# Encoder trunk on one core: neighbourhood values as one Strassen product, softmax division on ScalarE, two strips of w_out cut ahead

## The chip, the cores and the metric

The kernel runs on one core of one Trainium2 chip. Its engines are named as in the profile: PE is TensorE's matmul (PEld its weight load), DVE is VectorE, ACT is ScalarE, POOL is GpSimd, SP is SyncE, which here only issues DMAs. The metric is the device time of one launch in microseconds; lower is better.

## The reference

Two layers act on x, 256 rows of 2048 numbers. Each adds first a mixture of two attentions, then an MLP:

```
u = rmsnorm(x, norm_mix[l]);  proj = u @ w_in[l]
c_q, c_kv, k_pe, q_na, k_na, v_na, gate_a, gate_b = split(proj)
y_a = mla_attention(...) @ w_o_mla[l]                # 8 heads of latent attention, from c_q, c_kv, k_pe
y_b = neighbourhood_attention(q_na, k_na, v_na, rpb[l]) @ w_o_na[l]   # 8 heads of 128
x = x + (sigmoid(gate_a) * y_a + sigmoid(gate_b) * y_b) @ w_out[l]
x = x + square(relu(rmsnorm(x, norm_mlp[l]) @ w_ff1[l])) @ w_ff2[l]
```

and a last rmsnorm. Everything is float32. The values of the neighbourhood attention, `v_na`, are 1024 columns of `u @ w_in`, 128 for each of its 8 heads. A neighbourhood head computes scores from its queries and keys, adds a learned bias and a mask, takes a softmax over the 256 keys, and multiplies by its values.

## The kernel before

**A float32 product is made of three.** Every weight and activation is split into `hi`, rounded to the short float that TensorE multiplies (fp32r), and `lo`, the remainder; a product is hi x hi + lo x hi + hi x lo, three matmuls into one PSUM bank. ACT makes `hi` (lines 176 and 197), DVE `lo` (177 and 198). A weight is loaded as a block of 1 MB into one of 3 `raw` buffers by a DMA of SP. There are 8 PSUM banks, shared by all, and 51 slots of SBUF for activations.

**Kinds of product.** `gemm_b` gives 512 columns with the output turned, in 4 banks (lines 354, 359); `gemm_a` gives 512 columns by `group_a` (306, 310) in 2 banks, 16 row tiles x 2 x 3 = 96 matmuls of 128x512 where the input has 2048 columns; `gemm_s` (537) gives 1024 columns and runs over 8 pairs of row tiles, in the order `[0, 4, 1, 5, 2, 6, 3, 7]`. An ordinary pair costs 24 matmuls in 4 banks. Pairs 1, 2 and 3 (`MIXED`, `MERGED`) go by Strassen: 7 instead of 8 block products, 21 matmuls, in 7 banks. For that DVE forms `sums` of the weights (574 to 578), which are then split too, and `forms` prepares sums of the activations. At the end ACT and DVE put the quadrants together from the banks (587 and 586).

**The order.** The first layer runs `gemm_first` over all 1024 query columns of the neighbourhood part; the second layer makes the queries in two halves. Then, for each half of four heads: keys (`C_KN`, gemm_b), values (`C_VN`, two banks, `group_a`), and the four heads go into `queued`. Next come `C_Q`, `C_KV`, the rotary key, then the gates (`C_GB`, `C_GA`, gemm_s), `w_o_na`, the latent heads, `w_o_mla` (four gemm_a of 512 columns), `w_out` (two gemm_s) and the MLP.

**Heads run between products.** A head is a generator. Products call `tick()` now and then; every 6 ticks a queued head starts, and it yields between its steps: scores (three matmuls for each half, lines 314 to 316 in the old numbering, then `s` on DVE, 717), softmax (`nmx`, 650; exp on ACT, 658; `inv`, 662; the division `p` x `inv`, 664), 13 ticks later four transposes into a bank (669) and their split into `pp` on ACT and DVE (671, 672), 3 ticks later six value matmuls into another bank, split into `pair` (165, 167). A scheduler that orders each engine's instructions ahead of time has the last word, within the data's dependencies; at run time each engine takes its own list strictly in that order.

**Stores.** The first half of a layer uses `wpool` (4 buffers each of hi and lo, 1024 wide) and `tmp`; `half_a.close()` at line 910 gives both back before `w_out`, and `wpool2` (4 buffers, 2048 wide) with `tmp2` takes the space for `w_out` and the MLP.

## Time and profile before

| | |
|---|---|
| three runs | 2600.32, 2600.32, 2599.18 us; median 2600.32 |
| profiled run | 2599.52 us, of which the span (first to last instruction) is 2597.7 |
| PE busy | 2585.0 us, 100% of the span, 12432 matmuls |
| DVE busy | 2176.4 us, 84% |
| ACT busy | 1487.5 us, 57% |
| POOL busy | 98.0 us, 4% |
| read from HBM | 494.28 MB, 191 GB/s over the span |
| granted TensorE clock | 0.999 |

A page of the profile gives busy time by engine, the chain of work that ended last, and groups of equal instructions with the mean duration of one. Matmuls are pipelined, so the record of one is longer than its share of the engine. A group's line ends with the idle time of its engine just before it, and what ended that idle time. A row of the timeline has the start in us, the duration, engine, line, operation, output <- inputs, and, in brackets, the idle time before it and its releaser.

### The profile page before, as it was taken

What the parts mean: (1) busy time and instruction counts of PE and PEld (TensorE: products, weight loads), DVE (VectorE), ACT (ScalarE), POOL (GpSimd) and SP (SyncE); (2) the same over time, 40 slices, a digit from 0 to 9 for tenths busy, and PEclk for the clock granted to TensorE, in tenths of its full rate; (3) what the DMA queues carried; (4) which work ended last, traced back from release to release, by engine and by line L of the source; (5) the groups of instructions that cost most, each with busy time, mean ns of one, the idle gap of its engine ahead of it and who ended that gap; (6) DMA issues with size and microseconds to landing.
All of it is one profiled execution on the core that took longest, in us unless ns stands there. A gap on an engine that the chain in (4) does not pass through costs nothing.

```text
span 2597.7 us, 32260 instructions
## 1 busy us (share of the span) xinstructions
PE 2585.0 (100%) x12432; PEld 2171.9 (84%) x12432; DVE 2176.4 (84%) x2538; ACT 1487.5 (57%) x1732; POOL 98.0 (4%) x118
## 2 busy tenths in 40 slices
PE   9999999999999999999999999999999999999998
PEld 8888889888888888888888888898888888888887
DVE  7778889699988898888667788896999988988885
ACT  6555557456655645546545555574666556555463
POOL 0200000000000010000001000000000000100000
PEclk9999999999999999999999999999999999999999
DMA  7655564555577585675565555645656765856754
GB/s 266 217 171 195 180 205 151 165 191 195 195 219 220 176 259 198 202 239 171 178 201 178 173 194 182 205 149 161 197 180 211 234 199 192 246 194 209 243 180 145
DMA packets 173994, 511.06 MB, mean 197 GB/s; under 512 B 13840, under 2 KB 18832, under 8 KB 173584
## 3 DMA queue, kind: packets, MB, share of 16 engines
q1 hardware_dynamic: 164640, 491.78, 57.1%
q0 software_dynamic: 8768, 16.78, 3.3%
q8 instruction: 97, 1.59, 0.2%
q10 hardware_dynamic: 432, 0.43, 0.1%
q14 instruction: 57, 0.47, 0.1%
HBM read 494.28 MB, written 2.10 MB: 191 GB/s over the span
## 4 chain that ended last, share of the span: by engine, by line
PE 99%; issue 0%; ACT 0%; DVE 0%; POOL 0%; DVEq 0%; POOLq 0%; ACTq 0%
PE bank L537 67%; PE bank L306 8%; PE bank L354 6%; PE bank L310 4%; PE bank L359 3%; PE bank L285 2%; PE bank L507 1%; PE bank L260 1%; PE bank L286 1%; PE bank L314 1%; PE bank L316 1%; PE bank L315 1%; PE bank L258 1%; PE bank L669 1%; PE bank L605 0%
## 5 line engine op out<-in xcount | busy, mean ns | idle before, releaser
L537 PE MATMUL bank<-hi,pair 128*128 128x512 f32 x5124 | 1283.4, 390 | 2.1 <-ACT hi L176 2.1
L537 PEld LDWEIGHTS bank<-hi,pair 128*128 128x128 f32 x5124 | 958.0, 188 | 202.5 <-ACT hi L176 2.9
L176 ACT CAST hi<-raw 128x2048 fp32r<-128x2048 f32 (+3 forms) x416 | 622.7, 1517 | 301.7 <-PE bank L537 165.3
L177 DVE TENSOR_TENSOR lo<-raw,hi 128x2048 fp32r<-128x2048 f32 (+3 forms) x416 | 741.6, 1796 | 63.8 <-ACT hi L176 42.2
L537 PE MATMUL bank<-lo,pair 128*128 128x512 f32 x2562 | 697.2, 390 | 0.0
L537 PEld LDWEIGHTS bank<-lo,pair 128*128 128x128 f32 x2562 | 479.7, 188 | 99.4
L176 ACT CAST hi<-sums 128x2048 fp32r<-128x2048 f32 (+1 forms) x150 | 244.9, 1638 | 297.5 <-DVE sums L578 168.9
L177 DVE TENSOR_TENSOR lo<-sums,hi 128x2048 fp32r<-128x2048 f32 (+1 forms) x150 | 290.7, 1948 | 101.2 <-ACT hi L176 58.2
L198 DVE TENSOR_TENSOR lo<-raw,hi 128x1024 fp32r<-128x1024 f32 (+1 forms) x208 | 248.8, 1201 | 102.9 <-ACT hi L197 99.5
L197 ACT CAST hi<-raw 128x1024 fp32r<-128x1024 f32 (+1 forms) x208 | 214.1, 1035 | 205.0 <-PE bank L306 87.6
L306 PE MATMUL bank<-hi,pair 128*128 128x512 f32 x960 | 245.2, 392 | 0.0
L586 DVE TENSOR_TENSOR wide<-wide,bank 128x512 f32<-128x512 f32 x336 | 214.9, 679 | 6.5 <-PE bank L537 6.4
L306 PEld LDWEIGHTS bank<-hi,pair 128*128 128x128 f32 x960 | 178.3, 188 | 35.8
L354 PE MATMUL bank<-pair,hi 128*128 128x512 f32 x640 | 168.8, 395 | 0.0
L574 DVE TENSOR_TENSOR sums<-raw 128x1024 f32<-128x1024 f32 x126 | 153.7, 1220 | 13.9 <-DMA raw<-in_w_ff 7.3
L310 PE MATMUL bank<-lo,pair 128*128 128x512 f32 x480 | 131.9, 391 | 0.0
L354 PEld LDWEIGHTS bank<-pair,hi 128*128 128x128 f32 x640 | 112.4, 189 | 17.7
L310 PEld LDWEIGHTS bank<-lo,pair 128*128 128x128 f32 x480 | 89.4, 188 | 18.0
L516 ACT CAST pair<-wide 128x512 fp32r<-128x512 f32 x110 | 68.2, 620 | 59.8 <-DVE wide L475 57.5
L359 PEld LDWEIGHTS bank<-pair,lo 128*128 128x128 f32 x640 | 89.4, 190 | 7.2
L359 PE MATMUL bank<-pair,lo 128*128 128x256 f32 x640 | 93.7, 283 | 0.0
L578 DVE TENSOR_TENSOR sums<-raw,sums 128x512 f32<-128x512 f32 x126 | 86.6, 687 | 2.0
(165 smaller groups left out, 1890.7 us busy)
## 6 DMA issues: line engine op xcount, KB each, us to landing
raw<-in_w_ff SPq DMA_DIRECT2D x256, 1024.0 KB, 5.4
raw<-in_w_in SPq DMA_DIRECT2D x120, 1024.0 KB, 5.1
raw<-in_w_out SPq DMA_DIRECT2D x32, 1024.0 KB, 5.6
raw<-in_w_o_na SPq DMA_DIRECT2D x16, 1024.0 KB, 5.0
raw<-in_w_o_mla SPq DMA_DIRECT2D x16, 1024.0 KB, 5.0
xt<-wide POOLq DMA_DIRECT2D x48, 256.0 KB, 5.3
raw<-in_w_in SPq DMA_DIRECT2D x17, 512.0 KB, 5.6
raw<-in_w_ukv SPq DMA_DIRECT2D x8, 1024.0 KB, 5.0
```

Of the source, the lines that this page charges most:

```text
L176: nc.scalar.copy(hi, src)
L177: nc.vector.tensor_tensor(lo, src, hi.bitcast(F32), op=ALU.subtract)
L197: nc.scalar.copy(hi, src)
L198: nc.vector.tensor_tensor(lo, src, hi.bitcast(F32), op=ALU.subtract)
L306: nc.tensor.matmul(ps[t], a, wh[:, k], start=k0 + k + i == 0, stop=False)
L310: nc.tensor.matmul(ps[t], sides(have(acts, k0 + k), t)[0], wl[:, k], start=False, stop=k0 + k == nk - 1)
L354: nc.tensor.matmul(ps[m], wh[:, k, m * P:(m + 1) * P], have(acts, k0 + k), start=k0 + k == 0, stop=False)
L359: nc.tensor.matmul(ps[m][:, :S], wl[:, k, m * P:(m + 1) * P], have(acts, k0 + k)[:, :S], start=False, stop=k0 + k == nk - 1)
L537: nc.tensor.matmul(b[i], x, y, start=count[i] == 1, stop=count[i] == total[i])
L574: nc.vector.tensor_tensor(ts[0].rearrange("p (a n) -> p a n", a=2), raw[:, :512].rearrange("p (a n) -> p a n", a=1).to_broadcast([P, 2, 512]),
L578: final = nc.vector.tensor_tensor(t4, raw[:, 1536:], t2, op=ALU.subtract)
L586: add = lambda o, a, c: nc.vector.tensor_tensor(o, a, c, op=ALU.add)
```

## The change

Three edits.

1. **Values.** The two products `C_VN` of 512 columns become one `gemm_s` of 1024 columns with the pairs 1, 2, 3 by Strassen; `values` then reads the finished `wide` tiles instead of the banks. The values of all eight heads are made ahead of the second half of the keys. The `forms` of x, which the gates used first, move to the start of the layer; the loads of `xt` (the 2 MB of x, on SP) move behind the values.
2. **Division.** `p` x `inv` moves from DVE (`tensor_scalar_mul`) to ACT (a copy with a scale for each row).
3. **Strips ahead.** `cut` and the loading of a strip (`two_rows`) leave `gemm_s` and become functions of their own. A generator `strips_ahead`, started with the last `w_o_mla` product, closes `tmp`, opens a pool `wpool3` of two buffers on its space, and loads and cuts the first two strips of `w_out`; `gemm_s` takes them by its new argument `made`. From there on whole strips use `wpool3` and `wpool2` (2 buffers each) by turns, two strips from one, two from the other.

```diff
-        lo, hi = (wpool.tile([P, 2048 if strips else 1024], F32R, tag=tag, name=tag,
-                             bufs=hbufs)[:, :src.shape[-1]] for tag in ("lo", "hi"))
+        if strips:
+            whole_strips[0] += 1
+        pool, n, bufs = (stores[whole_strips[0] // 2 % 2], 2048, 2) if strips else (wpool, 1024, HBUFS)
+        hi, lo = (pool.tile([P, n], F32R, tag=tag, name=tag, bufs=bufs)[:, :src.shape[-1]] for tag in ("hi", "lo"))
...
+    def cut(src):
+        out, step = [], 2048 if strips else 1024
+        for c in range(0, src.shape[-1], step):
+            hi, lo = parts(src[:, c:min(c + step, src.shape[-1])])
+            out += [(hi[:, i:i + 512], lo[:, i:i + 512]) for i in range(0, hi.shape[-1], 512)]
+        return out
+
+    def two_rows(w, c0, j):
+        raw = raws.tile([P, 2048], F32, tag="raw", name="raw", bufs=RBUFS)
+        nc.sync.dma_start(raw.rearrange("p (k n) -> p k n", n=1024),
+                          w[2 * j * P:(2 * j + 2) * P, c0:c0 + 1024].rearrange("(k p) n -> p k n", p=P))
+        return raw
+
+    def gemm_s(w, c0, get, order, pairs, evac, made={}):
...
         first = next(j for j in order if j in pairs)
         for j in order:
-            raw = raws.tile([P, 2048], F32, tag="raw", name="raw", bufs=RBUFS)
-            nc.sync.dma_start(raw.rearrange("p (k n) -> p k n", n=1024),
-                              w[2 * j * P:(2 * j + 2) * P, c0:c0 + 1024].rearrange("(k p) n -> p k n", p=P))
+            raw = None if j in made else two_rows(w, c0, j)
             if j not in pairs:
-                ws = cut(raw)
+                ws = made[j] if j in made else cut(raw)
...
-            nc.vector.tensor_scalar_mul(p[:, b], p[:, b], inv[:, b:b + 1])
+            nc.scalar.activation(p[:, b], p[:, b], AF.Copy, scale=inv[:, b:b + 1])
...
+        qn, kn, xs4 = [None] * 8, [None] * 8, [None] * (NC // 2)
+
+        def put(norm, dst, g):
+            evac = to_pair(norm, dst)
+            return lambda m, ps: evac(g * 4 + m, ps)
+
+        def values_of(r):
+            return [[values(r[t, g], mix.col, t) for t in range(2)] for g in range(2)]
+
+        if l == 0:
+            gemm_first(wi, C_QN, xg, xf4, to_pair(None, qn), squared)
+            start(forms(xf4, MIXED, xs4), 8)
+            gemm_b(wi, C_KN, xg, put(mix, kn, 0), scaled, weights(wi, NC, C_KN, 512, tc.keep_in_program_order))
+            tables()
+        else:
+            start(forms(xf4, MIXED, xs4), 4)
+            gemm_b(wi, C_QN, xg, put(None, qn, 0), scaled)
+            gemm_b(wi, C_KN, xg, put(mix, kn, 0))
+        mixed, vt = blocks(xg, xs4, MIXED), []
+        gemm_s(wi, C_VN, mixed, ORDER, MIXED, lambda r: vt.extend(values_of(r)))
+        if l == 0:
+            for t in range(2):
+                tc.keep_in_program_order(nc.sync.dma_start(xt[t], x[t * P:(t + 1) * P]))
         for g in range(2):
-            qn, kn = (qn[4:] if l == 0 and g else [None] * 4), [None] * 4
-            if l == g == 0:
-                qn = [None] * 8
-                gemm_first(wi, C_QN, xg, xf4, to_pair(None, qn), squared)
-                gemm_b(wi, C_KN, xg, to_pair(mix, kn), scaled, weights(wi, NC, C_KN, 512, tc.keep_in_program_order))
-                tables()
-            else:
-                if l == 0:
-                    for t in range(2):
-                        tc.keep_in_program_order(nc.sync.dma_start(xt[t], x[t * P:(t + 1) * P]))
-                else:
-                    gemm_b(wi, C_QN + g * 512, xg, to_pair(None, qn), scaled if g == 0 else None)
-                gemm_b(wi, C_KN + g * 512, xg, to_pair(mix, kn))
-            ps = [bank() for _ in range(2)]
-            for k0, wh, wl in weights(wi, NC, C_VN + g * 512, 512):
-                group_a(ps, xg, k0, NC, wh, wl)
-                tick()
-            vt = [values(ps[t], mix.col, t) for t in range(2)]
-            for j in range(4):
-                h = g * 4 + j
-                queued.append(na_head(l, h, qn[j], kn[j], vt, mix.query, setter(att_na, h)))
+            if g:
+                if l:
+                    gemm_b(wi, C_QN + 512, xg, put(None, qn, 1))
+                gemm_b(wi, C_KN + 512, xg, put(mix, kn, 1))
+            for h in range(g * 4, g * 4 + 4):
+                queued.append(na_head(l, h, qn[h], kn[h], vt[g], mix.query, setter(att_na, h)))
...
+        half_b, made = ExitStack(), {}
+
+        def strips_ahead(l=l, made=made, half_b=half_b, heads_end=heads_end):
+            nonlocal strips
+            heads_end.close()
+            stores[0] = half_b.enter_context(tc.tile_pool(name="wpool3", bufs=2, side="right",
+                                                          reuse_waits="tile"))
+            whole_strips[0] = -1
+            for j in ORDER[:2]:
+                strips = True
+                made[j] = cut(two_rows(w_out[l], 0, j))
+                strips = False
+                if j == ORDER[0]:
+                    stores[0].tile([P, 56], F32, name="phase", bufs=1)
+                yield 1
...
+            if c4 == 3:
+                start(strips_ahead(), 7)
             gemm_a(w_o_mla[l], c4 * 512, att, merge)
...
+        while len(made) < 2:
+            tick()
         half_a.close()
...
-        wpool = half_b.enter_context(tc.tile_pool(name="wpool2", bufs=4, reuse_waits="tile"))
-        tmp = half_b.enter_context(tc.tile_pool(name="tmp2", bufs=2, reuse_waits="tile"))
+        wpool = stores[1] = half_b.enter_context(tc.tile_pool(name="wpool2", bufs=2, reuse_waits="tile"))
...
-            gemm_s(w_out[l], g * 1024, blocks(mg, ms4, MERGED), ORDER, MERGED, residual)
+            gemm_s(w_out[l], g * 1024, blocks(mg, ms4, MERGED), ORDER, MERGED, residual, {} if g else made)
```

In all, PE issues 18 matmuls of 128x512 fewer; 64 instructions move from DVE to ACT; 16 DMAs of 1 MB keep their bytes and change their shape. Three places show how the engines' lists move. In the names, `bank` is a PSUM bank and the number tells one tile from another; a wait in brackets names the engine or the DMA queue waited for.

**PE at the end of the second half of the keys, layer 0.** Before, `bank_999` to `bank_1002` are the key product, `pp_1220` and `bank_1271` belong to heads 1 and 2:

```order
L314 MATMUL bank_1241<-pp_1220,vh_989 128x256 [waits Activation_49]
L354 MATMUL bank_1002<-pair_458,hi_1263 128x512
L669 MATMUL bank_1271<-ident_71,p_1137 128x128 [waits DVE_49]
L669 MATMUL bank_1271<-ident_71,p_1137 128x128 x3
L354 MATMUL bank_999<-pair_461,hi_1263 128x512
L354 MATMUL bank_1000<-pair_461,hi_1263 128x512
L354 MATMUL bank_1001<-pair_461,hi_1263 128x512
L354 MATMUL bank_1002<-pair_461,hi_1263 128x512
L359 MATMUL bank_999<-pair_458,lo_1264 128x256
L359 MATMUL bank_999<-pair_461,lo_1264 128x256
L359 MATMUL bank_1000<-pair_458,lo_1264 128x256
L315 MATMUL bank_1241<-pp_1220,vh_989 128x256 [waits DVE_49]
```

Behind these follow the rest of head 1's value product and, between the next steps of heads 2 and 3, 21 more matmuls of the keys. In the changed kernel the same steps of heads 1 and 2, from the first row behind the keys' last matmul:

```order
L317 MATMUL bank_1461<-pp_1440,vh_1201 128x256 [waits Activation_49]
L676 MATMUL bank_1491<-ident_71,p_1357 128x128 [waits DVE_49]
L676 MATMUL bank_1491<-ident_71,p_1357 128x128 x3
L318 MATMUL bank_1461<-pp_1440,vh_1201 128x256 [waits DVE_49]
L319 MATMUL bank_1461<-pp_1440,vl_1202 128x256
L317 MATMUL bank_1461<-pp_1440,vh_1205 128x256
L318 MATMUL bank_1461<-pp_1440,vh_1205 128x256
L319 MATMUL bank_1461<-pp_1440,vl_1206 128x256
L317 MATMUL bank_1517<-pp_1496,vh_1201 128x256 [waits Activation_49]
L318 MATMUL bank_1517<-pp_1496,vh_1201 128x256 [waits DVE_49]
L319 MATMUL bank_1517<-pp_1496,vl_1202 128x256
L317 MATMUL bank_1517<-pp_1496,vh_1205 128x256
```

Behind these stand two more value matmuls of head 2, the first transpose of head 3, which waits for ACT, and then the first matmul of C_Q. The matmuls of the key product that stood between the heads' steps are now ahead of them. In layer 1 the same fifteen rows stand behind the second half of the queries, and similar ones behind the second half of the keys.

**DVE at the same place.** Before, with head 3's scores `s_1200`:

```order
L717 SCALAR_TENSOR_TENSOR s_1200<-bank_1193,query_647,mb_1189 128x256 [waits DMASW6_49,DMASW7_49,PE_49,Pool_49]
L717 SCALAR_TENSOR_TENSOR s_1200<-bank_1193,query_647,mb_1189 128x256
L650 TENSOR_REDUCE nmx_1203<-s_1200 128x2 [waits DVE_49]
L167 TENSOR_TENSOR pair_1182<-bank_1175,pair_1182 128x256 [waits Activation_49]
L198 TENSOR_TENSOR lo_1366<-raw_1363,hi_1365 128x1024 [waits DMAHW7_49,PE_49]
L672 TENSOR_TENSOR pp_1220<-bank_1215,pp_1220 128x2x256 [waits Activation_49]
L662 RECIPROCAL inv_1209<-sm_1206 128x2 [waits Activation_49]
L664 TENSOR_SCALAR p_1205<-p_1205,inv_1209 128x256 [waits DVE_49]
L664 TENSOR_SCALAR p_1205<-p_1205,inv_1209 128x256
```

and after, with head 3's scores `s_1420`, where `small_1551` and its like empty the banks of the keys:

```order
L724 SCALAR_TENSOR_TENSOR s_1420<-bank_1413,query_647,mb_1409 128x256 [waits DMASW6_49,DVE_49,DMASW7_49,PE_49,Pool_49]
L168 TENSOR_TENSOR pair_1402<-bank_1395,pair_1402 128x256 [waits Activation_49]
L724 SCALAR_TENSOR_TENSOR s_1420<-bank_1413,query_647,mb_1409 128x256
L679 TENSOR_TENSOR pp_1440<-bank_1435,pp_1440 128x2x256 [waits Activation_49]
L657 TENSOR_REDUCE nmx_1423<-s_1420 128x2 [waits DVE_49]
L201 TENSOR_TENSOR lo_1711<-raw_1688,hi_1710 128x1024 [waits PE_49,Activation_49]
L325 TENSOR_TENSOR small_1551<-bank_1219,small_1549 128x256 [waits Activation_49]
L679 TENSOR_TENSOR pp_1496<-bank_1491,pp_1496 128x2x256 [waits Activation_49]
```

The two divisions of each head are gone from the list; `pp_1496`, which PE's row with `bank_1517` waits for, stands behind the evacuation of head 0 (`pair_1402`), the row maximum, a split of C_Q's weights (`lo_1711`) and the first emptying of the keys' banks.

**ACT at the start of w_out, layer 0.** Before, the first strip (`hi_5123`) comes behind all that belongs to the merged blocks:

```order
L197 CAST hi_5091<-raw_5064 128x1024 [waits PE_49]
L165 ACTIVATE pair_5039<-bank_5034 128x256 [waits PE_49]
L165 ACTIVATE pair_5042<-bank_5034 128x256 [waits DVE_49]
L165 ACTIVATE pair_5054<-bank_5049 128x256 [waits PE_49]
L165 ACTIVATE pair_5057<-bank_5049 128x256 [waits DVE_49]
L176 CAST hi_5123<-raw_5120 128x2048 [waits DMAHW4_49]
L176 CAST hi_5177<-raw_5174 128x2048 [waits DMAHW5_49]
```

After (`hi_5140` and `hi_5151` are the two strips ahead, `hi_5113` and `hi_5155` the last block of `w_o_mla`):

```order
L200 CAST hi_5073<-raw_5055 128x1024 [waits PE_49]
L179 CAST hi_5140<-raw_5138 128x2048 [waits DMAHW4_49]
L618 ACTIVATE wide_4984<-bank_4979 128x256 [waits PE_49]
L618 ACTIVATE wide_4984<-bank_4979 128x256
L166 ACTIVATE pair_4987<-wide_4984 128x256 [waits Activation_49]
L200 CAST hi_5113<-raw_5111 128x1024 [waits DMAHW3_49,PE_49]
L166 ACTIVATE pair_4990<-wide_4984 128x256 [waits Activation_49]
L618 ACTIVATE wide_5002<-bank_4997 128x256 x2
L166 ACTIVATE pair_5005<-wide_5002 128x256 [waits Activation_49]
L166 ACTIVATE pair_5008<-wide_5002 128x256 [waits Activation_49]
L200 CAST hi_5155<-raw_5111 128x1024 [waits PE_49]
L179 CAST hi_5151<-raw_5149 128x2048 [waits DMASW5_49,DMASW4_49,DMASW6_49,DMASW3_49,DMASW7_49,DMASW2_49,DMAHW5_49,DMASW1_49,DMASW0_49]
```

The first strip's cast moved ahead of the last two casts of `w_o_mla`, the second ahead of the last four blocks' `pair`.

More of the change, by code (lines that the diff above doesn't have):

```diff
@@ L86, in trunk @@
     hbufs, smalls, strips = HBUFS, SMALL, False
+    stores, whole_strips = [None, None], [-1]
     def bank():
@@ L522, in turned_pair @@
         yield
-    def gemm_s(w, c0, get, order, pairs, evac):
+    def cut(src):
[10 more added lines that the diff above has]
+    def gemm_s(w, c0, get, order, pairs, evac, made={}):
         b, count, total = {}, {}, {i: 0 for i in range(1, 9)}
@@ L546, in products @@
                 mm(i, ah, wl)
-        def cut(src):
-            out, step = [], 2048 if strips else 1024
-            for c in range(0, src.shape[-1], step):
-                hi, lo = parts(src[:, c:min(c + step, src.shape[-1])])
-                out += [(hi[:, i:i + 512], lo[:, i:i + 512]) for i in range(0, hi.shape[-1], 512)]
-            return out
         first = next(j for j in order if j in pairs)
         for j in order:
-            raw = raws.tile([P, 2048], F32, tag="raw", name="raw", bufs=RBUFS)
-            nc.sync.dma_start(raw.rearrange("p (k n) -> p k n", n=1024),
-                              w[2 * j * P:(2 * j + 2) * P, c0:c0 + 1024].rearrange("(k p) n -> p k n", p=P))
+            raw = None if j in made else two_rows(w, c0, j)
             if j not in pairs:
-                ws = cut(raw)
+                ws = made[j] if j in made else cut(raw)
                 ah, al = get(j)
@@ L755, in trunk @@
         wpool = half_a.enter_context(tc.tile_pool(name="wpool", bufs=4, reuse_waits="tile"))
-        tmp = half_a.enter_context(tc.tile_pool(name="tmp", bufs=2, reuse_waits="tile"))
+        heads_end = ExitStack()
+        tmp = heads_end.enter_context(tc.tile_pool(name="tmp", bufs=2, reuse_waits="tile"))
         wi = w_in[l]
@@ L816, in trunk @@
         start(nq.scales(False), 10)
-        xs4 = [None] * (NC // 2)
-        start(forms(xf4, MIXED, xs4), 10)
         gemm_b(wi, C_KV, xg, lambda m, ps: whole(ps, held[m]))
@@ L842, in local @@
             gemm_a(w_o_na[l], c4 * 512, att_na, merge)
-        mixed = blocks(xg, xs4, MIXED)
         gemm_s(wi, C_GB, mixed, ORDER, MIXED, gate(part, 0))
@@ L909, in trunk @@
                 start(forms(mf4, MERGED, ms4), 4)
+        while len(made) < 2:
+            tick()
         half_a.close()
         last = l == DEPTH - 1
-        half_b = ExitStack()
         strips = True
-        wpool = half_b.enter_context(tc.tile_pool(name="wpool2", bufs=4, reuse_waits="tile"))
-        tmp = half_b.enter_context(tc.tile_pool(name="tmp2", bufs=2, reuse_waits="tile"))
+        wpool = stores[1] = half_b.enter_context(tc.tile_pool(name="wpool2", bufs=2, reuse_waits="tile"))
         mlp = RowNorm()
```

## The prediction

> **What bounds the kernel now.** I read the page's first and fourth part, then the longest pieces of the chain, then the waits of PE, then four windows.
>
> ```profile
> span 2597.7 us, 32260 instructions
> PE 2585.0 (100%) x12432; PEld 2171.9 (84%) x12432; DVE 2176.4 (84%) x2538; ACT 1487.5 (57%) x1732; POOL 98.0 (4%) x118
> PE 99%; issue 0%; ACT 0%; DVE 0%; POOL 0%; DVEq 0%; POOLq 0%; ACTq 0%
> 280.00 114.51 PE bank L537 x505
> PE bank L537 <- ACT hi L176: 2.1, 2, 1.0
> ```
>
> The first three lines say that TensorE is the bound: it is busy over the whole span, and the chain that ended last is PE for 99%. A matmul record lasts longer than its share of the engine, so busy time does not give the price of one; the fourth line does: 505 of the 128x512 matmuls follow each other in 114.51 us, **0.2267 us each**. The fifth, from the waits of PE, is the whole of what the wide products wait for: twice, 2.1 us together. So only two things can shorten this kernel, fewer matmuls and those two waits, and everything that makes PE wait anew lengthens it.
>
> The windows (columns: window, its length, then busy us and count of PE, PEld, DVE, ACT, POOL, clock, DMA share, GB/s) show how much cover the other engines have.
>
> ```profile
> 96.00:125.40 29.40, 29.40 (x189) 26.50 (x188) 23.23 (x41) 17.49 (x35) 10.01 (x12) 1.00 0.57 180
> 206.20:246.90 40.70, 40.70 (x181) 33.62 (x181) 33.92 (x42) 24.05 (x29) 0.00 (x0) 1.00 0.58 203
> 250.00:526.00 276.00, 275.73 (x1398) 234.51 (x1396) 223.68 (x339) 157.76 (x250) 0.69 (x1) 1.00 0.53 176
> ```
>
> The first lies in the neighbourhood part of layer 0, the second is one gate product by `gemm_s`, the third runs from there to the end of the last `w_o_mla` product. PE has no gap in the first two and 0.27 us in 276 in the third.
>
> **The change part by part. Values as one product.** Two products of 512 columns cost 2 x 96 = 192 matmuls of 128x512. One `gemm_s` of 1024 columns with three of eight row pairs by Strassen costs 5 x 24 + 3 x 21 = 183. Two layers: 18 matmuls fewer, 18 x 0.2267 = **4.08 us off PE**, all of it on the path. What comes with it (sums of weights, more hi/lo, eight more `wide` additions) is DVE and ACT work. I cost it at nothing in its own stage, for the second window is a product of the same shape, order and pairs: 33.92 us of DVE and 24.05 of ACT lie beside 40.70 of PE without a gap. If that cover were gone, DVE would still need 6.8 us more before it were the longer one. The handover of banks at the end of such a product is in the third window three times, again without a gap; and the bytes are the same, 16 DMAs in another shape for 16, with `xt` behind them on SP instead of ahead. The `forms` of x, moved ahead, cost 3 small groups a layer, beside the key product; the same groups of the merged blocks lie hidden in the third window.
>
> **Strips ahead.** At the start of `w_out` stands the only wait of size.
>
> ```profile
> 523.06 0.38 ACT L165 ACTIVATE pair<-bank 128x256 fp32r<-128x256 f32 x1 [8.35 <-PE bank L605]
> 523.47 0.42 DVE L169 SCALAR_TENSOR_TENSOR pair<-bank,pair 128x256 fp32r<-128x256 f32 x1 [5.42 <-ACT pair L165]
> ...
> 525.26 1.07 PE L310 MATMUL bank<-lo,pair 128*128 128x512 f32 x4
> 525.42 3.71 ACT L176 CAST hi<-raw 128x2048 fp32r<-128x2048 f32 x2
> 527.37 0.50 PE L537 MATMUL bank<-hi,pair 128*128 128x512 f32 x1 [1.04 <-ACT hi L176]
> ...
> 1818.13 1.07 PE L310 MATMUL bank<-lo,pair 128*128 128x512 f32 x4
> 1820.24 0.50 PE L537 MATMUL bank<-hi,pair 128*128 128x512 f32 x1 [1.04 <-ACT hi L176]
> ```
>
> The last four matmuls of `w_o_mla` start at 525.26 and take 4 x 0.2267 = 0.91; the next would start at 526.17 and starts at 527.37, when ACT has cut the first strip. That is 1.20 us, and 1820.24 - 1819.04 = 1.20 in layer 1: **2.40 us go** if the strips are there. Room for them: ACT idles 8.35 us and DVE 5.42 us just before, in one stretch each, and two strips cost two of each of these:
>
> ```profile
> L177 DVE TENSOR_TENSOR lo<-raw,hi 128x2048 fp32r<-128x2048 f32 x186 | 423.7, 2286 | 48.0 <-ACT hi L176 35.3 <-PE bank L537 12.3
> L176 ACT CAST hi<-raw 128x2048 fp32r<-128x2048 f32 x186 | 353.5, 1913 | 95.1 <-PE bank L537 62.3 <-DMA raw<-in_w_ff 18.0 <-PE bank L306 8.3
> ```
>
> 2 x 1.91 = 3.8 on ACT and 2 x 2.29 = 4.6 on DVE. The first cast now stands on ACT ahead of the last two casts of `w_o_mla` and waits for its own DMA; if that lands late, those two and the transposed blocks queue up behind it. Late next is the first Strassen strip of `w_out` (sums, then casts); before, it came behind two strips cut late, so it has more time now. Bounds of this part: 0 and 2.4 us gained.
>
> **Division on ScalarE.** 64 instructions go from DVE to ACT.
>
> ```profile
> L664 DVE TENSOR_SCALAR p<-p,inv 128x256 f32<-128x256 f32 x64 | 23.1, 404 | 0.6
> L165 ACT ACTIVATE pair<-wide,g_sb 128x256 fp32r<-128x256 f32 x24 | 11.0, 500 | 1.3 <-DMA wide<-in_x_turned 1.3
> L165 ACT ACTIVATE pair<-bank 128x256 fp32r<-128x256 f32 x52 | 19.3, 380 | 34.0 <-PE bank L605 17.1 <-PE bank L316 10.5 <-DVE pair L169 6.4
> ```
>
> DVE loses 64 x 0.404 = 25.9 us of records. ACT with a per-row scale is not shown on `p`; the same form on 128x256 with a scale column takes 0.50, without one 0.38, so I take the nearer, 64 x 0.50 = 32 us (24 by the other), on an engine that is 57% busy. Off the path that costs nothing; where PE waits for a head it is 0.10 us a half longer, and a step between engines is added (DVE, ACT, PE instead of DVE, PE). The Trainium skill (ScalarE: Activation LUTs, section Rules for kernel authors) says of a `mul` to use VectorE, not ScalarE, which speaks against this edit; the two rows agree in sign, 404 against 500 ns. The same page (What ACT_TABLE_LOAD costs) gives an ACTIVATE 186 ns + 0.833 per element and 93 for a pointer operand, an estimate of 492 ns for 256 elements; the trace's 500 is used. By that rule a version with the division left on VectorE would come out some 0.1 us at each of four waits, 0.4 us, below my sum.
>
> **Where heads wait.** The values of heads 0 to 3 now exist before the second half of the keys, and those heads run in that product (in layer 1 in the second half of the queries). Their banks are the eight that the product and the next one use too. PE's order puts the ends of the head chains behind the product's last matmul, three times: behind KN's second half in layer 0 and QN's second half in layer 1 (the same 15 rows, place A) and behind KN's second half in layer 1 (place B); and, thinner, behind C_Q in layer 0 (place C). Before, the same rows have product matmuls between them:
>
> ```profile
> 169.99 0.60 PE L669 MATMUL bank<-ident,p 128*128 128x128 f32 x4
> 170.34 1.18 PE L354 MATMUL bank<-pair,hi 128*128 128x512 f32 x4
> 171.30 0.69 DVE L672 TENSOR_TENSOR pp<-bank,pp 128x512 fp32r<-128x512 f32 x1 [0.74 <-ACT pp L671]
> 171.70 0.28 PE L315 MATMUL bank<-pp,vh 128*128 128x256 f32 x1
> 172.18 0.28 PE L316 MATMUL bank<-pp,vl 128*128 128x256 f32 x1
> 172.92 0.42 DVE L167 TENSOR_TENSOR pair<-bank,pair 128x256 fp32r<-128x256 f32 x1 [0.93 <-ACT pair L165]
> 173.26 1.22 DVE L198 TENSOR_TENSOR lo<-raw,hi 128x1024 fp32r<-128x1024 f32 x1
> 174.05 0.28 PE L314 MATMUL bank<-pp,vh 128*128 128x256 f32 x1
> ```
>
> From these: four transposes take 170.34 - 169.99 = 0.35; 128x256 matmuls follow at (172.18 - 171.70)/4 = 0.12; between a head's transposes (170.59) and its value product (174.05) PE had over 3 us of other work, and no wait. Now it has 0.6. What DVE must do meanwhile, by means:
>
> ```profile
> L198 DVE TENSOR_TENSOR lo<-raw,hi 128x1024 fp32r<-128x1024 f32 x192 | 233.7, 1222 | 101.1 <-ACT hi L197 97.9 <-PE bank L310 2.4
> L322 DVE TENSOR_TENSOR small<-bank,small 128x256 f32<-128x256 f32 x80 | 30.8, 414 | 0.0
> L672 DVE TENSOR_TENSOR pp<-bank,pp 128x512 fp32r<-128x512 f32 x32 | 21.9, 686 | 4.2 <-ACT pp L671 4.0
> L717 DVE SCALAR_TENSOR_TENSOR s<-bank,query,mb 128x256 f32<-128x256 f32 x32 | 13.9, 477 | 4.4 <-issue 4.4
> L695 DVE TENSOR_TENSOR small<-small,rrow 128x256 f32<-128x256 f32 x32 | 13.5, 441 | 0.0
> L167 DVE TENSOR_TENSOR pair<-bank,pair 128x256 fp32r<-128x256 f32 x32 | 13.4, 419 | 14.0 <-ACT pair L165 14.0
> L650 DVE TENSOR_REDUCE nmx<-s 128x2 f32<-128x512 f32 x16 | 10.9, 684 | 0.3
> L662 DVE RECIPROCAL inv<-sm 128x2 f32<-128x2 f32 x32 | 5.0, 156 | 0.3
> L671 ACT CAST pp<-bank 128x512 fp32r<-128x512 f32 x32 | 18.9, 589 | 14.6 <-PE bank L669 14.5
> L658 ACT ACTIVATE p<-s,nmx 128x256 f32<-128x256 f32 x32 | 16.0, 503 | 3.1 <-DVE nmx L650 3.1
> ```
>
> Place A, from the moment when the first half of head 3's scores is in its bank. DVE's queue: s, pair, s, pp, nmx, lo, small, pp = 0.477 + 0.419 + 0.477 + 0.686 + 0.684 + 1.222 + 0.414 + 0.686 = 5.07 us; neighbours in the queue start 0.08 closer than a record lasts (172.92 to 173.26, a record of 0.42), so 8 x 0.08 less, 4.4. PE until it needs that last `pp`: 3 x 0.12 of scores, 0.35 of transposes, 2 x 0.2267 + 8 x 0.12 of the product's rest, 0.35 of transposes, 7 x 0.12 of value products = 3.3. It waits 1.1 to 1.8; I take 1.3. Behind it, the first transpose of head 3 waits for the division: small, small, inv on DVE and one half on ACT, 0.414 + 0.441 + 0.156 + 0.50 = 1.5 (1.3 with the overlap), against 5 x 0.12 = 0.6 on PE; I take 0.7. Together 2.0 at each of the two places A. Place B has s, s, nmx, pp, pair, lo, inv, small, pp on DVE, 5.2 by means and 4.5 with the overlap, against 3.9 on PE: 1.0, and 0.6 for the division: 1.6. Place C: 0.3, since C_Q's last matmuls and C_KV's first stand among the rows. Sum 2 x 2.0 + 1.6 + 0.3 = **5.9 us**. Bounds: nothing, if PE is fed as it was before; and by means throughout, with both halves of the division waited for, 2 x 3.2 + 3.0 + 1.0 = 10.4.
>
> **The sum**, against the profiled run of 2599.52 us (span 2597.7 and what lies around it; 0.8 us under the median of 2600.32, within the three runs): 2599.52 - 4.08 - 2.40 + 5.9 = 2598.9, said as **2599.0**.
>
> **The rivals.** A measurement of this kernel tells about 0.2%, 5.2 us, from no change; counted from the median the bounds are 2595.1 and 2605.5.
>
> First, the heads cost next to nothing, under 2.1 us. For it: the window at 96 us has heads beside a product with no gap, and DVE is freed of 26 us of divisions. Against: there PE had other work. It gives 2599.52 - 6.48 + 0.5 = 2593.5, faster. Chance 0.28.
>
> Second, the other side: the last head of a batch runs alone. If the product behind cannot start until head 3 (or 7) has given its banks back, PE stands through its chain at each of the four places: s, nmx, two exp, inv, two divisions, transposes, pp on ACT and on DVE, 0.477 + 0.684 + 2 x 0.503 + 0.156 + 2 x 0.50 + 0.35 + 0.589 + 0.686 = 4.9 us, 20 in all, 2613 us. It decides from 12.5 us of waits, 3.1 a place. For it: four banks of the ended product are still being emptied there, and ACT now carries exp, division, casts and copies in one queue. Against: PE's order puts only one of head 3's transposes ahead of C_Q's first matmul. Chance 0.08.
>
> Third, the change does not do what it says at `w_out`: the wait moves behind the two strips, to the first Strassen strip, since its store opens only when the old pools close, or a late first DMA holds up ACT. Then 2.4 us stay: 2601.4. Against: SP issues the first of the two right behind the last load of `w_o_mla`. Chance 0.09.
>
> The forecast itself, waits of 2.1 to 10 us: chance 0.55. **Range** 2592.5 to 2604.5: it takes in the first and third rival and nearly the upper bound of the waits (2603.4). Faster 0.28, same 0.55 + 0.09 = 0.64, slower 0.08.
>
> **What would show it.** In the changed profile: the wait of PE on the hi cast at `w_out` gone from both layers; the value product some 41.5 us long with no gap; and PE gaps of 1 to 2 us at the ends of products in the neighbourhood part of each layer, released by DVE `pp` and by ACT `p`. If those gaps are absent, the time is near 2593.5 and my place A is wrong; if each is over 3 us, the second rival holds. If `wide` additions or weight sums release PE anywhere, the cover that I took from the gate product is not there.

## The result, and the profile after

The change makes the kernel slower: 2634.26 us median (2633.73 to 2635.5, 4 runs) against 2599.89 us (2599.18 to 2600.32, 4 runs) beside it, a ratio of 1.0133, 95% interval 1.0116 to 1.0151. I had forecast 2599.0 and a range up to 2604.5.

The same parts of the page, and the first rows of the waits of PE, now read:

```profile
span 2632.2 us, 32266 instructions
PE 2599.5 (99%) x12414; PEld 2169.6 (82%) x12414; DVE 2194.6 (83%) x2520; ACT 1520.3 (58%) x1810; POOL 93.3 (4%) x118
PE 93%; ACT 3%; DVE 3%; issue 1%; DMA 0%; DVEq 0%; ACTq 0%; POOLq 0%; POOL 0%
...
PE bank L553 <- ACT hi L179: 7.4, 8, 1.3
PE bank L553 <- DVE lo L180: 4.3, 2, 2.6
PE bank L553 <- ACT pair L519: 3.4, 10, 0.4
PE bank L318 <- DVE pp L679: 2.3, 2, 1.1
...
PE bank L676 <- ACT p L671: 1.0, 2, 0.6
```

PE has 18 matmuls fewer (12414 for 12432), as planned, and yet the chain that ended last is ACT for 3% and DVE for 3%, where it had been PE throughout. The waits of the wide products (L553, gemm_s) on ACT's `hi` were 2.1 us and are now 7.4, with 4.3 on DVE's `lo`, which before had none, and 3.4 on the activations' `pair` beside them.

To see where, I took the start of each stage from the trace (the first matmul that reads a strip of the stage's weights) and subtracted:

| stage, us | before, layer 0 / 1 | after, layer 0 / 1 | difference |
|---|---|---|---|
| layer's start to w_o_na (neighbourhood part, first gate) | 242.0 / 240.6 | 245.4 / 242.3 | +3.5, +1.6 |
| w_o_na to w_out (gates, latent heads, w_o_mla) | 280.7 / 280.7 | 279.4 / 279.4 | -1.3, -1.3 |
| w_out to the first w_ff2 (w_out, first w_ff1) | 171.2 / 171.2 | 184.1 / 185.7 | +12.9, +14.5 |
| first w_ff2 to the layer's end | 600.3 / 597.3 | 602.5 / 599.6 | +2.2, +2.3 |

The wait at the start of w_out went, as forecast (it stood ahead of w_out's first matmul, so it counts in the row above). But behind it, where w_out runs into the MLP, 27.4 us came in two stretches of 171 us. The windows of these stretches, before (two rows) and after (two rows):

```profile
527.30:698.60 171.30, 171.21 (x781) 141.58 (x782) 163.18 (x167) 108.76 (x113) 2.93 (x1) 1.00 0.60 197
1820.20:1991.50 171.30, 171.24 (x781) 141.62 (x782) 163.25 (x167) 108.71 (x112) 2.93 (x1) 1.00 0.60 197
```

```profile
529.60:713.80 184.20, 177.66 (x792) 143.32 (x791) 166.30 (x178) 109.49 (x116) 0.69 (x1) 0.99 0.54 182
1837.90:2023.60 185.70, 178.23 (x791) 143.34 (x790) 166.41 (x178) 109.56 (x116) 0.69 (x1) 0.99 0.55 180
```

About the same matmuls, about the same work on DVE and ACT, a lower DMA share: nobody had much more to do. Eight more `lo` matmuls stand in the second pair (244 for 236, counted by line): they came behind the first w_ff2 matmul before and come ahead of it now, so 8 x 0.2267 = 1.8 us of each difference moved here from the row below it, and the loss is 11.1 and 12.7 us here and some 4 us in each of the two stretches behind. PE is idle for 6.5 and 7.5 us, against 0.1 before; a lower granted clock (0.99 for 1.00, see the last section) takes another 1.7 us of each. The rest I did not assign row by row. So somebody waited longer. ACT's casts of strips show for what; first the group's row of before, then of after:

```profile
L176 ACT CAST hi<-raw 128x2048 fp32r<-128x2048 f32 (+3 forms) x416 | 622.7, 1517 | 301.7 <-PE bank L537 165.3
```

```profile
L179 ACT CAST hi<-raw 128x2048 fp32r<-128x2048 f32 (+1 forms) x448 | 653.8, 1478 | 467.6 <-PE bank L553 310.1
```

A cast that waits for PE waits for a strip buffer that PE still reads. That idle time grew from 165 to 310 us. (With the values changed and no split store, below, it is 178.) ACT is not the bound, so idle time there costs nothing by itself; it costs where the strip comes too late, as here in layer 0 (timeline; in brackets the idle time before the instruction and its releaser):

```profile
557.68 3.71 ACT L179 CAST hi<-raw 128x2048 fp32r<-128x2048 f32 x2 [2.38 <-PE bank L553]
559.64 0.73 PE L553 MATMUL bank<-hi,pair 128*128 128x512 f32 x2 [1.11 <-ACT hi L179]
```

ACT stands 2.38 us until PE gives a buffer back, casts, and PE stands until the cast is done. Lining up each engine's list with the trace gives the names of these strips. Numbered as they are cut, with the start of the cast and the last matmul that reads `hi`:

```
strip              before: tile, cast, last read      after: tile, store, cast, last read
4 (Strassen sums)  hi_5235  536.42  557.43            hi_5282  wpool2  535.42  557.21
5                  hi_5266  538.24  546.09            hi_5313  wpool3  533.60  551.10
6                  hi_5300  540.60  549.95            hi_5347  wpool3  540.00  552.00
7 (Strassen sums)  hi_5304  546.70  558.11            hi_5351  wpool2  549.99  557.90
8                  hi_5331  548.52  556.29            hi_5378  wpool2  557.68  563.16
```

From cast to last read strip 4, of sums, holds its buffer for 21 us in both kernels; the others hold theirs for 8 to 11 before, and for 5 to 18 after. Before, strip 8 took whichever buffer was free, at 548.52, while strip 4 was still held: six later strips passed by it through the other three buffers. After, strip 8 belongs to `wpool2` by its turn, and both buffers there hold sums, until 557.21 and 557.90. One buffer of `wpool3` stood empty from 552.0 to 561.3. The wait of 1.11 us is one of many; the largest piece, 7 of the 11.1 us of layer 0, comes between 632 and 655 us, where w_out hands over to the MLP (windows of after):

```profile
640.00:645.00 5.00, 3.74 (x15) 2.03 (x13) 2.66 (x7) 4.97 (x7) 0.69 (x1) 1.00 0.61 204
...
650.00:655.00 5.00, 2.90 (x11) 1.55 (x10) 4.85 (x6) 3.80 (x6) 0.00 (x0) 1.00 0.21 43
```

That is the theory to test: **four buffers are still there, but two and two by turns are not four.**

In the neighbourhood part the values are what they were forecast to be, and the places A look as forecast too (window of the value product; then PE rows at place A of layer 0, and of layer 1):

```profile
74.50:115.10 40.60, 40.60 (x181) 33.64 (x180) 34.93 (x44) 23.92 (x32) 1.42 (x1) 1.00 0.68 248
```

```profile
145.77 0.39 PE L318 MATMUL bank<-pp,vh 128*128 128x256 f32 x1 [1.13 <-DVE pp L679]
147.05 0.33 PE L676 MATMUL bank<-ident,p 128*128 128x128 f32 x1 [0.43 <-ACT p L671]
...
1433.54 0.39 PE L318 MATMUL bank<-pp,vh 128*128 128x256 f32 x1 [1.13 <-DVE pp L679]
```

No gap in 40.60 us of values; a wait for `pp` of DVE and one for the division on ACT at the end of the chains.

### The profile page after: what moved, and what is told of

It reads as the page before. It is cut to its first block, busy times and chain, and to the rows that moved or that the text cites. A ratio compares the mean times of both kernels' runs of the same rounds, so it can differ in the third digit from the quotient of the medians.

```text
span 2632.2 us, 32266 instructions
## 1 busy us (share of the span) xinstructions
PE 2599.5 (99%) x12414; PEld 2169.6 (82%) x12414; DVE 2194.6 (83%) x2520; ACT 1520.3 (58%) x1810; POOL 93.3 (4%) x118
## 4 chain that ended last, share of the span: by engine, by line
PE 93%; ACT 3%; DVE 3%; issue 1%; DMA 0%; DVEq 0%; ACTq 0%; POOLq 0%; POOL 0%
PE bank L553 65%; PE bank L309 6%; PE bank L357 6%; PE bank L313 3%; PE bank L362 3%; ACT hi L179 2%; PE bank L288 2%; PE bank L510 1%; PE bank L263 1%; PE bank L289 1%; PE bank L317 1%; PE bank L319 1%; PE bank L318 1%; PE bank L261 1%; DVE lo L180 1%
## 5 line engine op out<-in xcount | busy, mean ns | idle before, releaser
L553 PE MATMUL bank<-hi,pair 128*128 128x512 f32 x5368 | 1346.7, 392 | 12.6 <-ACT hi L179 7.4
L553 PEld LDWEIGHTS bank<-hi,pair 128*128 128x128 f32 x5368 | 1001.9, 188 | 234.7 <-ACT hi L179 10.8
L179 ACT CAST hi<-raw 128x2048 fp32r<-128x2048 f32 (+1 forms) x448 | 653.8, 1478 | 467.6 <-PE bank L553 310.1
L180 DVE TENSOR_TENSOR lo<-raw,hi 128x2048 fp32r<-128x2048 f32 (+1 forms) x448 | 780.4, 1753 | 95.1 <-ACT hi L179 74.2
L553 PE MATMUL bank<-lo,pair 128*128 128x512 f32 x2684 | 724.1, 391 | 4.4 <-DVE lo L180 4.3
L553 PEld LDWEIGHTS bank<-lo,pair 128*128 128x128 f32 x2684 | 503.5, 188 | 111.3 <-DVE lo L180 6.3
L180 DVE TENSOR_TENSOR lo<-sums,hi 128x2048 fp32r<-128x2048 f32 (+1 forms) x162 | 305.4, 1895 | 113.8 <-PE bank L553 63.7
L179 ACT CAST hi<-sums 128x2048 fp32r<-128x2048 f32 (+1 forms) x162 | 257.5, 1594 | 244.6 <-PE bank L553 122.2
L201 DVE TENSOR_TENSOR lo<-raw,hi 128x1024 fp32r<-128x1024 f32 (+1 forms) x176 | 211.2, 1209 | 64.1 <-ACT hi L200 56.9
L200 ACT CAST hi<-raw 128x1024 fp32r<-128x1024 f32 (+1 forms) x176 | 180.1, 1032 | 122.0 <-PE bank L309 47.4
L593 DVE TENSOR_TENSOR wide<-wide,bank 128x512 f32<-128x512 f32 x352 | 226.4, 682 | 6.6 <-PE bank L553 6.4
L313 PE MATMUL bank<-lo,pair 128*128 128x512 f32 x352 | 96.1, 391 | 0.0
L585 DVE TENSOR_TENSOR sums<-raw,sums 128x512 f32<-128x512 f32 x132 | 90.9, 689 | 2.0
L584 DVE TENSOR_TENSOR sums<-raw,sums 128x512 f32<-128x512 f32 x132 | 90.7, 687 | 0.9
```

Source lines behind the costliest of these rows:

```text
L179: nc.scalar.copy(hi, src)
L180: nc.vector.tensor_tensor(lo, src, hi.bitcast(F32), op=ALU.subtract)
L200: nc.scalar.copy(hi, src)
L201: nc.vector.tensor_tensor(lo, src, hi.bitcast(F32), op=ALU.subtract)
L313: nc.tensor.matmul(ps[t], sides(have(acts, k0 + k), t)[0], wl[:, k], start=False, stop=k0 + k == nk - 1)
L553: nc.tensor.matmul(b[i], x, y, start=count[i] == 1, stop=count[i] == total[i])
```

## Experiments

Three theories stood for the 34 us: the split store (S), cutting ahead as such (A), and the values as one product (V). The change without strips ahead, the split store alone, the first strip in the old store and the values alone ran on one chip beside 22 runs of the kernel before (2599.79 us), the four pieces on another beside 11 (2599.72), the rest on a third beside 27 (2599.58).

**The change without strips ahead.**

```diff
-        pool, n, bufs = (stores[whole_strips[0] // 2 % 2], 2048, 2) if strips else (wpool, 1024, HBUFS)
+        lo, hi = (wpool.tile([P, 2048 if strips else 1024], F32R, tag=tag, name=tag,
+                             bufs=hbufs)[:, :src.shape[-1]] for tag in ("lo", "hi"))
...
-                start(strips_ahead(), 7)
...
-        wpool = stores[1] = half_b.enter_context(tc.tile_pool(name="wpool2", bufs=2, reuse_waits="tile"))
+        wpool = half_b.enter_context(tc.tile_pool(name="wpool2", bufs=4, reuse_waits="tile"))
...
```

> The change without its third edit: values as one product and division on ScalarE stay, w_out and the MLP use one store of four buffers again and no strip is cut ahead. Three theories for the 34 us: (S) the store of four, split into two of two taken by turns, makes a strip wait for its own store while a buffer of the other is free; (A) cutting strips ahead does it, by what it puts in front on ScalarE and SP; (V) the values as one product do it, by shifting what follows. From the stage lengths of the two traces the part up to w_o_na is 3.5 us (layer 0) and 1.6 us (layer 1) longer in the change. S and A: 2599.9 + 3.5 + 1.6 = 2605, w_out with its wait of 1.2 us back. V: 2630 or more.

Measured: 2604.28 us (2602.86 to 2604.93, 11 runs), ratio 1.0016, interval 1.0007 to 1.0025. V falls: 30 us of the 34 leave with the third edit. w_out to the first w_ff2 is back at 171.4 and 171.2 us.

**The split store alone, in the kernel before.**

```diff
+        pool, n, bufs = (stores[whole_strips[0] // 2 % 2], 2048, 2) if strips else (wpool, 1024, HBUFS)
...
-        wpool = half_b.enter_context(tc.tile_pool(name="wpool2", bufs=4, reuse_waits="tile"))
+        stores[0] = half_b.enter_context(tc.tile_pool(name="wpool3", bufs=2, reuse_waits="tile"))
+        wpool = stores[1] = half_b.enter_context(tc.tile_pool(name="wpool2", bufs=2, reuse_waits="tile"))
```

> The kernel before with one thing changed: the whole strips of w_out and the MLP go by turns, two and two, into two stores of two buffers, both opened where the one of four was; nothing is cut ahead. S: most of the loss is here, 25 to 32 us, 2625 to 2632, and ScalarE's casts idle for PE far longer than the 165 us of before. A and V: 2600.

Measured: 2629.89 us (2629.38 to 2630.44, 4 runs), ratio 1.0116, interval 1.0102 to 1.013. S holds, and A falls as the cause of the 30 us: nothing is cut ahead here, and the loss is all there. Its group of casts and its waits of PE:

```profile
L179 ACT CAST hi<-raw 128x2048 fp32r<-128x2048 f32 (+3 forms) x416 | 624.3, 1517 | 441.2 <-PE bank L540 291.6
...
PE bank L540 <- DVE lo L180: 9.3, 4, 3.9
PE bank L540 <- ACT hi L179: 6.0, 4, 2.9
```

ACT's idle time for PE goes from 165.3 to 291.6 us with this edit alone. The waits are not the whole price. In the stretches from w_out to the first w_ff2 the granted clock (third number from the end) falls as well:

```profile
529.90:711.50 181.60, 177.12 (x788) 145.89 (x789) 163.91 (x171) 108.59 (x112) 0.69 (x1) 0.97 0.58 191
1838.20:2019.20 181.00, 176.56 (x788) 145.28 (x789) 163.77 (x171) 108.66 (x113) 0.69 (x1) 0.98 0.59 192
```

Against 1.00 before, 0.03 x 181.6 + 0.02 x 181.0 is some 9 of the 30 us, by these rounded shares.

**Four buffers in one store, in strict turns.** Is it the two stores, or the turn?

```diff
...
+        n, bufs, turn = (2048, 1, str(whole_strips[0] % 4)) if strips else (1024, hbufs, "")
+        lo, hi = (wpool.tile([P, n], F32R, tag=tag + turn, name=tag, bufs=bufs)[:, :src.shape[-1]] for tag in ("lo", "hi"))
```

> The kernel before with the same four strip buffers in one store, but strip n must use buffer n mod 4 instead of any that is free. S sharpened: it is the fixed turn that costs, not that there are two stores; with no choice left at all the loss is at least that of the split store: 2630 to 2645. If two stores as such cost (their places in SBUF), this stays at 2600.

Measured: 2636.07 us (2633.67 to 2636.59, 4 runs) against 2599.58, ratio 1.0137, interval 1.0122 to 1.0153. One store, four buffers, no choice: 36 us. So it is the turn that costs, and with no choice at all a little more than with a choice of one in two. One thing stays open: the scheduler also wrote other lists for the engines (in the table above, strip 5 is cut ahead of strip 4 after the change). No kernel here has the old lists with fixed turns, so the 30 us are the price of both together. Of its waits of PE the longest stand again behind DVE's `lo` of a late strip:

```profile
PE bank L540 <- DVE lo L180: 13.7, 6, 4.9
```

**The first strip in the old store.** Can the 2.4 us be had without a split?

```diff
+            if opening and j == order[1]:
+                opening()
...
```

`opening` closes the stores of the first half and opens `wpool2` with 4 buffers; the call stands between the first strip and the second.

> The kernel before, but the first strip of w_out is loaded and cut in two halves in the store of the first half of the layer, before that store is closed; then one store of four as before. S: the wait at the start of w_out goes at no cost elsewhere, 2 x 1.2 us, 2597.5. A: no gain or a loss, 2600 or more, since the casts now stand ahead of the last transposed blocks on ScalarE.

Measured: 2607.84 us (2606.72 to 2608.59, 6 runs), ratio 1.0031, interval 1.0019 to 1.0042. A miss for S; A's bound, 2600 or more, holds. No wait for ACT's `hi` is left at the start of w_out, and yet w_out to the first w_ff2 takes 176.9 and 179.4 us instead of 171.2. A named the place wrongly, though: PE's waits lie at the end of w_out, not at the casts ahead. The first strip in four pieces, below, shows it more closely.

**Values alone, the division back on DVE.**

```diff
-            nc.scalar.activation(p[:, b], p[:, b], AF.Copy, scale=inv[:, b:b + 1])
+            nc.vector.tensor_scalar_mul(p[:, b], p[:, b], inv[:, b:b + 1])
```

> The first edit alone: values as one product, division on VectorE, one store of four. Against the change without strips ahead this tells what the division on ScalarE is worth in this order of heads. If PE's waits at the ends of the head chains are set by the division on ScalarE (my 0.7 us of 2.0 at each place), about 2 to 3 us faster than it: 2602 to 2603. If VectorE's queue sets them, the divisions put back there make them longer: 2606 to 2608.

Measured: 2603.12 us (2602.19 to 2604.58, 11 runs), ratio 1.0013, interval 1.0004 to 1.0022. About 1 us under the version with the division on ACT, with overlapping runs: not settled by this pair which engine matters there, and not my 2 to 3 us.

**The division alone, in the kernel before** (the same line, the other way round).

> The kernel before with the division on ScalarE and nothing else. Theory H: what costs time in the neighbourhood part is the place where PE's list holds only head steps (rows of transposes and value products with no product between), and the engine of the division matters only there; this kernel has no such stretch of 14 rows or more in PE's list. H: 2599 to 2600.5. Rival D: the step through ScalarE costs by itself, 0.1 us a half and a hand-over for each of 32 heads: 2603 or more.

Measured: 2599.6 us (2599.11 to 2600.6, 11 runs) against 2599.58, ratio 0.9999, interval 0.9991 to 1.0008. Off the path the division on ACT costs nothing that can be measured; D falls.

**The rotary key's product between the keys and C_Q**, values as one product, division on DVE, one store:

```diff
             gemm_b(wi, C_QN, xg, put(None, qn, 0), scaled)
+            gemm_b(wi, C_QN + 512, xg, put(None, qn, 1))
...
                 gemm_b(wi, C_KN + 512, xg, put(mix, kn, 1))
...
+                ps = bank()
+                for k0, wh, wl in weights_twice(wi, NC, C_KPE, ROPE):
+                    for k in range(8):
+                        mm_b(ps, wh[:, k], wl[:, k], xg[k0 + k], k0 + k == 0, k0 + k == NC - 1)
+                        tick()
...
```

The first line added is layer 1's: its second half of the queries moves ahead of the values, together with the first. The old places of both products are taken out.

> Values as one product, division on VectorE, one store of four; and the small product of the rotary key (32 matmuls, one bank, about 5.5 us) is moved between the second half of the keys and C_Q, in layer 1 both halves of the queries come first. So the tails of heads 0 to 3 fall into a product that takes one bank instead of four, and PE's list has no head-only stretch of 14 rows. H: most of the 8 us between 2603.1 and 2599.8 - 4.1 = 2595.7 comes back: 2596 to 2598.5, faster than the kernel before. Rival B: the waits come from the eight heads being later than before whatever lies between: 2601 to 2603.

Measured: 2598.23 us (2597.69 to 2598.71, 11 runs), ratio 0.9994, interval 0.9985 to 1.0003. That is 4.9 us under the values alone, with the same operations: the waits came from what lies between the heads' steps, and B falls. What is left of them:

```profile
PE bank L551 <- ACT hi L177: 2.1, 2, 1.0
PE bank L315 <- ACT pp L676: 1.7, 2, 0.8
```

The first row is w_out's old wait; the second, two waits of 0.8 us, is what is left at the heads. How much each of the two moved products did was not tried apart. Against the kernel before the interval still holds 1, so it is not shown to be faster.

**The same with the division on ACT.**

> The same with the division on ScalarE. PE's list has again a head-only stretch of 17 rows in each layer, behind the second half of the keys. H: slower than the version with the division on VectorE by some 2 us a stretch, 2599 to 2602. B: the same as it.

Measured: 2601.32 us (2599.83 to 2602.28, 11 runs), ratio 1.0005, interval 0.9996 to 1.0014; 3.1 us over the version with DVE, their runs apart. As H had it: the same edit that costs nothing in the kernel before costs here, where its order leaves PE a list of head steps only. By the stages of the two profiled runs, up to w_o_na 242.6 us against 241.6 in layer 0 and 241.0 against 239.8 in layer 1, it lies in the neighbourhood part; the spans differ by 1.7 us. The medians differ by more, because six of the eleven runs with ACT also show a lower granted clock (last section).

**The first strip cast in four pieces**, on the version with the rotary key between, and alone in the kernel before:

```diff
+        for c in (512, 0, 1536, 1024) if fine[0] else ():
+            nc.scalar.copy(hi[:, c:c + 512], src[:, c:c + 512])
...
```

> The version with the rotary key between (2598.2), and the first strip of w_out cast on ScalarE in four pieces of 512 columns, in the order in which TensorE uses them, instead of one of 2048. No store, DMA or strip moves; TensorE can start after the first piece, 0.62 us instead of 1.91. Of the wait of 1.20 us in each layer 1.1 to 1.2 go: 2595.8 to 2596.2, faster than the kernel before by 0.14%. Rival O: the order of w_out is so tight that any edit there costs some us at the hand-over to the MLP, as with the first strip in the old store: 2600 to 2606.

> The same four pieces in the kernel before, nothing else. 2599.7 - 2.3 = 2597.4. O: 2602 to 2608.

Measured: 2607.31 us (2606.62 to 2607.92, 7 runs), ratio 1.0029, interval 1.0018 to 1.004; and 2609.15 us (2606.28 to 2609.82, 5 runs), ratio 1.0034, interval 1.0021 to 1.0047, both against 2599.72. O holds in kind; both times lie above its ranges (2600 to 2606, 2602 to 2608). In the second of them the start of w_out is what I wanted, and the price comes 110 us later (timeline):

```profile
525.75 2.17 ACT L178 CAST hi<-raw 128x512 fp32r<-128x512 f32 x4
526.50 1.85 PE L542 MATMUL bank<-hi,pair 128*128 128x512 f32 x7
...
637.22 0.72 PE L542 MATMUL bank<-lo,pair 128*128 128x512 f32 x2 [1.64 <-DVE lo L182]
639.80 0.80 PE L542 MATMUL bank<-hi,pair 128*128 128x512 f32 x1 [1.39 <-ACT pair L521]
```

and the window around the second place:

```profile
635.00:640.00 5.00, 1.97 (x8) 1.03 (x7) 4.90 (x5) 4.47 (x4) 2.92 (x1) 0.90 0.55 174
```

PE starts w_out without a wait at 526.50 and stands at 637 and 639 in the first product of the MLP, busy for 1.97 of 5 us, while DVE is busy for 4.90. No instruction was added there. What differs is the order that the scheduler wrote for PE, ACT and DVE: with w_out starting earlier it put the last reads of two strips of sums later (the first two of w_out's second product are read until 609.6 and 610.3, before until 603.3 and 603.9), the next strip gets its buffer at 609.6 instead of 605.0, and DVE then has their `lo` and the start of the MLP to do at once. The version with the first strip in the old store has the same late reads, at 609.5 and 610.2. That this is the cause is argued from these reads; I made no kernel that holds the old order and starts early, so it stays open.

## Why the prediction was wrong

**The step that failed** is "Strips ahead". It priced the cutting (3.8 us of ACT and 4.6 of DVE into idle time) and the wait that goes, and gave as bounds "0 and 2.4 us gained". The other half of the same edit, the store of four that becomes two of two by turns, has no term in the sum at all: I read 2 + 2 as 4. The runs put it at 30 us alone (split store alone, +30.1) and 30 us within the change (2634.26 against 2604.28 without it). The profile of before held a number that could have warned me: ACT's casts already idled 165 us for PE to give buffers back, so the store had little to spare; with the choice gone, part of the longer wait reached PE. Without the third edit the rest of the same sum, 2599.52 - 4.08 + 5.9, gives 2601.3, and 2604.28 was measured.

**The third rival** looked at this place, for a wait that moves to the first Strassen strip, at 2.4 us; and the second, "slower" rival looked at the heads. Neither had the store.

**Values as one product**: right as far as the runs show it. 18 matmuls fewer, 40.60 us of the product without a gap, DVE at 34.93 where I had 33.92 from the gate product. The 4.08 us themselves were not measured apart from the heads.

**The wait at the start of w_out**: right, 2.4 us, and w_o_na to w_out is 1.3 us shorter in each layer. But the three kernels that removed it without a split store lost more behind it (8.1, 7.6 and 9.4 us against the kernel before), so none of them shows the 2.4 us as a gain.

**Heads**: right in mechanism and place, too small in sum. Counted from stage lengths, 3.5 + 1.6 and the 4.1 of the matmuls saved, 9.2 us against my 5.9. PE's waits there come to 4.7 us by the records, so the first rival, heads at next to nothing, falls. Place A is near what I worked out in layer 0 (1.13 and 0.43 us against 1.3 and 0.7); in layer 1 it has the 1.13 alone. Place B has 0.45 and 0.57 for my 1.6. Place C was put at 0.3 and has a wait of 0.74 for `small` and one of 0.25 for `pp`. One price was not in the sum, the clock (below), 1.7 us in layer 0. The other 2.8 of the 9.2 us stand in no row of waits, and their cause stays open. That these waits hang on what lies between was shown by the version with the rotary key's product between.

**Division**: right off the path, 0.0 us alone, and right in its price, 0.50 us by the nearest row; the group in the changed kernel:

```profile
L671 ACT ACTIVATE p<-p,inv 128x256 f32<-128x256 f32 x64 | 29.2, 508 | 1.5 <-DVE inv L669 1.5
```

At the heads the medians of the two engines differ by 1 us in one order and 3 us in another; part of both is the clock.

## What to carry to other kernels

A number of buffers is not the whole of a store: what counts is how many strips can pass one that is held long, so before splitting a store, or fixing turns in it, look at how long its filler already idles for the reader, and at how far apart the longest and the shortest use lie (here 21 and 8 us). Where an engine's order is written ahead by a scheduler, an edit that starts a stage 1 us earlier may change the order of everything behind it, so time the stages and not only the place that was mended. And a chain of small steps costs nothing while other work lies between its rows on the bound engine: here, moving the rotary key's product, and in layer 1 half of the queries, brought back 4.9 us.

## What the runs showed of the hardware

PE's granted clock fell after waits much shorter than I would have feared. In the changed kernel, three rows of windows around place A of layer 0 (the clock is the third number from the end):

```profile
143.00:147.10 4.10, 2.44 (x18) 1.84 (x17) 4.10 (x11) 3.71 (x13) 1.84 (x3) 1.00 0.44 96
147.10:150.90 3.80, 3.80 (x13) 3.19 (x14) 3.42 (x10) 2.04 (x6) 0.47 (x1) 0.55 0.59 224
150.90:155.00 4.10, 4.10 (x28) 3.67 (x27) 0.73 (x2) 1.52 (x2) 0.00 (x0) 1.00 0.00 0
```

PE is busy for 2.44 of 4.10 us, with gaps of 1.13 and 0.43 us as the longest, and then runs 3.8 us at a granted clock of 0.55, which costs about 1.7 us (0.45 x 3.8) that appear in no row of waits. It happens twice more, in the stretches from w_out into the MLP; in layer 0 (0.34 x 5, again 1.7 us):

```profile
645.00:650.00 5.00, 4.76 (x15) 3.69 (x15) 5.00 (x8) 2.24 (x5) 0.00 (x0) 0.66 0.00 0
```

and in the first product of the MLP with the first strip in four pieces:

```profile
640.00:645.00 5.00, 5.00 (x12) 3.93 (x13) 5.00 (x7) 2.46 (x6) 0.00 (x0) 0.50 0.68 219
645.00:650.00 5.00, 5.00 (x21) 4.05 (x20) 4.27 (x8) 3.36 (x5) 0.00 (x0) 0.91 0.28 111
```

There 12 matmuls take the 5 us in which 22 would run; with the window before (0.90, shown above) and the one behind it costs (0.10 + 0.50 + 0.09) x 5 = 3.4 us, twice the 1.7. It does not come each time: the change without strips ahead has the same waits for `pp` (its waits of PE, then a window) and kept its clock:

```profile
PE bank L316 <- DVE pp L677: 2.3, 2, 1.1
```

```profile
146.00:150.00 4.00, 3.57 (x22) 2.97 (x21) 4.00 (x13) 2.73 (x7) 1.01 (x1) 1.00 0.68 243
```

That is its profiled run, of 2602.88 us. Of its eleven runs five have a mean granted clock of 0.999 and take 2602.86 to 2603.64 us, the other six have 0.998 and take 2604.28 to 2604.93. The two groups lie some 1.4 us apart, which fits one more drop of the clock in the slower six; no trace of those runs is kept, so that is argued. The version with the rotary key between and the division on ACT is split in the same way, 2599.83 to 2600.67 and 2601.32 to 2602.28.

The Trainium skill (TensorE: Matmul & The Clock Gate, section Why this matters for your kernels) asks for no idle gaps of PE over about 3 us between bursts; here gaps of at most 1.13 us, together 1.66 us in 4.10, were enough, sometimes. So a cluster of short waits should be priced with 1.7 us on top, or twice that, as a chance and not as a certainty.
